# Six buffers of split weights and the two parts of a normed input, placed at other SBUF addresses

## The chip, the cores and the metric

The kernel runs on one core of one Trainium2 chip. The metric is device microseconds (us) of one execution; lower is better. The kernel before takes 1207.95 us, the median of three runs (1205.56 to 1208.57). All data are float32, and the output has to agree with a float32 reference.

## What is computed

One decoder layer on 512 tokens of 1024 features, with a memory of 256 tokens. The reference, cut to its skeleton:

```python
def mixing_sublayer(h, mem_n, ...):
    z = h @ w_in                                  # 1024 -> 9472 columns
    xa, ga, q, k, v, us, xq, gates = jnp.split(z, SPLIT_IDX, axis=-1)
    ya = rg_lru_branch(xa, ga, ...)               # conv, gates, linear scan
    yb = dilated_attention(q, k, v)               # 3 groups of 4 heads
    yc = s5_branch(us, ...)                       # complex diagonal SSM, GLU
    yx = memory_cross_attention(xq, mem_n, mem_wkv)
    g = jax.nn.sigmoid(gates.reshape(B_, L, N_BRANCH, D_MODEL))
    m = (g[:, :, 0] * (ya @ proj_a) + g[:, :, 1] * (yb @ proj_b)
         + g[:, :, 2] * (yc @ proj_c) + g[:, :, 3] * (yx @ proj_x))
    return m @ w_out
def conv_gated_mlp(h, w_up, conv_w, conv_b, w_down):
    up = h @ w_up                                 # 1024 -> 6144
    gate = causal_dwconv(up[..., D_FF:], conv_w, conv_b)
    return (up[..., :D_FF] * jax.nn.gelu(gate)) @ w_down
# reference: x = x + rms_norm(mixing(rms_norm(x))); x = x + rms_norm(mlp(rms_norm(x)))
```

## The kernel before

**Exact products from two parts.** Every large matrix product is made of float32 operands that are split into a high part, rounded to the width of one TensorE pass (type float32r), and a low part, the rest. A product of 128 output features by 512 tokens over a 128-wide slice of the contraction is three matmuls: high weights by low input, high weights by high input, low weights by high input. `mm3` (L82 to L92) writes them in this order for each of 8 slices (6 for a 768-wide contraction), so that a *unit* is 24 (or 18) matmuls of 512 columns into one PSUM bank. In `mm3` the stationary operand, which TensorE loads before a matmul, is a 128x128 slice of the weights, and the moving operand, which it streams, is a 128x512 slice of the input.

**Weights.** `wfetch` (L70) lets SyncE's queue bring 512 KB of weights into a buffer `wraw`. `wload` (L75) makes the two parts: ScalarE copies them to `whi` (L79) and VectorE subtracts (L80) to give `wlo`. Each of the three has three buffers, which rotate, in the pool `wp`; so there are six buffers of split weights, of 128 partitions x 4096 bytes.

**Inputs.** The normed input, turned so that features are on partitions, is `hT`: two tiles `hTh` and `hTl` of 8 x 512 tokens (L178). All 74 units of `w_in` read it as moving operand (names xa, ga, us, xq, q, k, v and gate in the rows). The branches' outputs `ya`, `yx`, `gy`, `yc`, `yb` are pairs of such tiles as well; `merge` (L269) takes them through the projections (prj), each after the unit of its gate: a tile of `merge` is 24 + 18 matmuls (24 + 6 for `yb`). The GLU of the S5 branch reads `gy`. The MLP's first product (`up`, L779) reads `h2h` and `h2l`. Its second (`dn`, L837) turns the roles round: the stationary operand is a slice of `aTh` or `aTl`, and the moving one the split weights; the same holds of `w_out` (`wo`, L699).

**Order.** The program's instructions are written in one order for all engines and each engine runs its own in that order; buffers that come free release the next transfer or copy. Small tiles of 128x512 come from a ring `t2` of six buffers.

**Addresses.** A tile gets its address from its pool when the program is built: pools stand one behind the other in each partition's SBUF, in steps of 32 bytes. The addresses below are read from the built programs, in bytes within a partition, modulo 512. A unit's slices are 512 bytes (weights) and 2048 bytes (input) apart, so a whole tile has one such residue.

Of the kernel before, what the change touches and what calls it, by code (L numbers as in the profile page):

```python
# [12 lines left out]
F32 = mybir.dt.float32  # L13
F32R = mybir.dt.float32r
# [4 lines left out]
PSUM = bass.MemoryType.PSUM  # L19
# [31 lines left out]
def _body(ctx, tc, nc, D):  # L51
    cp = ctx.enter_context(tc.tile_pool(name="cp", bufs=1))
    wp = ctx.enter_context(tc.tile_pool(name="wp", bufs=3))
    ps = ctx.enter_context(tc.tile_pool(name="ps", bufs=4, space=PSUM))
# [19 lines left out]

    def wload(src, n, raw=None):  # L75
        raw = wfetch(src, n) if raw is None else raw
        hi = wp.tile([128, 1024], F32R, tag="whi", name="whi")
        lo = wp.tile([128, 1024], F32R, tag="wlo", name="wlo")
        S.copy(hi[:, :n], raw[:, :n])  # L79
        V.tensor_tensor(out=lo[:, :n], in0=raw[:, :n], in1=f32(hi[:, :n]), op=ALU.subtract)  # L80
        return hi, lo

    def mm3(out, w, x, nk):
        """out[128, N] = sum over nk chunks of w_k^T x_k, operands given as exact hi + lo parts."""
        whi, wlo = w
        n = 0
        for k in range(nk):
            sl = slice(k * 128, (k + 1) * 128)
            for a, b in ((whi, 1), (whi, 0), (wlo, 0)):
                last = PE.matmul(out, a[:, sl], x[b][:, k], start=(n == 0), stop=(n == 3 * nk - 1))  # L90
                n += 1
        return last  # L92

    def split(hi, lo, src, scale=None, eng=V):
        """hi + lo = src (* scale), hi rounded to the width of one pass."""
        if scale is None:
            a = S.copy(hi, src)
            b = eng.tensor_tensor(out=lo, in0=src, in1=f32(hi), op=ALU.subtract)  # L98
        else:
            a = S.activation(hi, src, AF.Identity, scale=scale)  # L100
            b = V.scalar_tensor_tensor(out=lo, in0=src, scalar=scale, in1=f32(hi), op0=ALU.mult, op1=ALU.subtract)
        return a, b
# [11 lines left out]
    def rstd_of(pool, s0, s1, n, tag, bufs=1, between=None, eng=V):  # L114
        """((s0 + s1) / DM + EPS) ** -0.5, with a Newton step after the table's root; between() goes beside the root."""
        t, y, e, r = (pool.tile([128, n], F32, tag=tag + x, name=tag + x, bufs=bufs) for x in "tyer")
        if s1 is None:
            eng.tensor_scalar(out=t, in0=s0, scalar1=EPS * DM, scalar2=None, op0=ALU.add)
        else:
            eng.tensor_scalar(out=t, in0=s0, scalar1=s1, scalar2=EPS * DM, op0=ALU.add, op1=ALU.add)  # L120
        S.activation(y, t, AF.Sqrt, scale=1.0 / DM)
        if between is not None:
            between()
        V.reciprocal(y, y)
        if n == 1:
            eng.tensor_scalar(out=e, in0=y, scalar1=y, scalar2=t, op0=ALU.mult, op1=ALU.mult)
        else:
            eng.tensor_tensor(out=e, in0=y, in1=y, op=ALU.mult)
            eng.tensor_tensor(out=e, in0=e, in1=t, op=ALU.mult)
        eng.tensor_scalar(out=e, in0=e, scalar1=-0.5 / DM, scalar2=1.5, op0=ALU.mult, op1=ALU.add)  # L130
        eng.tensor_tensor(out=r, in0=y, in1=e, op=ALU.mult)
        return r
# [28 lines left out]
    def turned_rows(xs, gain, dst, k0, k1):  # L161
        """dst[k] (hi, lo) <- xs turned to have features on partitions, times gain."""
        for k in range(k0, k1):
            b = axb("nT")
            for t in range(4):
                PE.transpose(b[:, t * 128:(t + 1) * 128], xs[t][:, k * 128:(k + 1) * 128], ident)
            last = split(dst[0][:, k, :], dst[1][:, k, :], b, scale=gain[:, k:k + 1])
        return last

    mp = ctx.enter_context(pool("mp"))  # L170
    # the memory's keys of a head's whole chunks (0 .. 3) and, with the other head's rows at zero, shared ones (4 .. 7)
# [6 lines left out]
    hT = (hp.tile([128, KC, L], F32R, name="hTh"), hp.tile([128, KC, L], F32R, name="hTl"))  # L178
# [16 lines left out]
    with pool("np") as npool:  # L195
# [9 lines left out]
        # the rows' scale comes after the products  # L205
# [14 lines left out]
        ones, dg = npool.tile([128, 128], F32, name="ones"), npool.tile([128, 2, 128], F32, name="dg")  # L220
# [65 lines left out]
    ya = ynew("ya")  # L286
    with pool("lru", bufs=2) as lp, pool("lruc") as lc:
# [5 lines left out]
        with tc.issue_after(normed[0].ins), tc.issue_after(normed[1].ins):  # L293
            for b in (ba, bx):
                V.tensor_scalar(out=b, in0=b, scalar1=0.5, scalar2=None, op0=ALU.mult)
            # softplus(-lam) = max(-lam, 0) + log1p(e), e = exp(-|lam|), by the series of 2 atanh(e / (2 + e))
# [152 lines left out]
    apx = ExitStack()  # L449
    ap = apx.enter_context(pool("at"))  # L450
    sel0 = ap.tile([2, 128], F32, name="selh")
# [4 lines left out]
    # order of the tokens in a group: 4 tiles of 128  # L456
# [12 lines left out]
    class Attention:  # L469
        """Two heads of each group."""  # L470

        def __init__(self, h2):
# [7 lines left out]
            # maxima in columns 0 and 1, sums in 32 and 33  # L480
# [20 lines left out]
        def units_k(self, g):  # L501
            b = unit(U_K + 2 * g + self.h2, "k")
            # each head's keys, the other head's rows at zero
# [63 lines left out]
        def weigh(self):  # L567
            # weights of the groups, per head and token: exp(m_g - M) / sum_g exp(m_g - M) l_g
# [40 lines left out]
        def run(self, fill, before=None):  # L609
            """The group's steps between products that don't wait for them; before() comes with the first."""  # L610
# [69 lines left out]
    with pool("wo") as wo:  # L680
# [93 lines left out]
        # the first products of the MLP in halves of the tokens, the first of which are there sooner  # L774
# [69 lines left out]
    # the last products by tiles of tokens, whose weights stand where h2 did  # L844
# [32 lines left out]
def s5_params(nc, tc, D, keep_pool, pool):  # L877
    V, S = nc.vector, nc.scalar
    r = {}
    with pool("s5t") as tp:  # L880
# [29 lines left out]
        def exp(o, x):  # L910
            """exp(x) = 2^n exp(r): the power of two from the table, rid of its error by its mantissa's bits, times a polynomial."""
# [31 lines left out]
        # z = (A - 1) / lambda  # L943
# [26 lines left out]
        # powers of A  # L970
# [8 lines left out]
        # a chunk's decay, and the powers 0 .. 15 and 0, 16 .. 112 of its rotation  # L979
# [25 lines left out]
class S5:  # L1005
    """S5 in batches of eight groups (four pairs) over 128 chunks of 4 tokens: lanes are (group of the pair, state)."""
# [12 lines left out]
    def tables(self, i):  # L1019
        """The rotations R^c of the chunks, and V_j = A^(3 - j) B."""  # L1020
# [33 lines left out]
    def prepare(self, i):  # L1054
        """The batch's matrices: inputs to chunk sums, states to outputs, inputs to outputs within a chunk."""
# [7 lines left out]
        # inputs: [(j, group of the pair, h), pair, chunk]  # L1063
# [3 lines left out]
        # W_n = C A^n  # L1067
# [14 lines left out]
        # K_tau = Re(C A^tau B), tau = 0 .. 3, with D on its first diagonal  # L1082
# [55 lines left out]
    def states(self, i):  # L1138
        """The batch's states before each chunk."""
# [7 lines left out]
        # sums of a chunk's inputs, turned back by its rotation  # L1147
# [19 lines left out]
        # states before each chunk  # L1167
# [12 lines left out]
    def outputs(self, i):  # L1180
        """GELU of the batch's outputs, chunks on partitions."""
        S, PE, st = self.nc.scalar, self.nc.tensor, self.b[i]
        U, (xr, xi) = st["U"], st["x"]
        # y: [chunk, pair, (group, j, h)]
# [9 lines left out]
    def turned(self, i):  # L1194
        """The same with features on partitions, tokens in (j, c) order, in a bank of PSUM."""
# [70 lines left out]
```

## Time and profile before

| what | before |
|---|---|
| median of three runs | 1207.95 us |
| span of the profiled execution | 1209.4 us |
| PE busy, share of the span | 1181.5 us, 98% |
| DVE, ACT, POOL busy | 685.4, 516.8, 132.4 us |
| granted TensorE clock, mean | 0.995 |
| DMA, mean | 99 GB/s |

The span of the profiled execution lies 1.45 us above the median of the runs. Engines: PE is TensorE (PEld its weight loads), DVE VectorE, ACT ScalarE, POOL GpSimd, SP SyncE. Matmuls overlap, and the end of one is modelled, so its duration (0.39 us here) says little. What it costs is the *gap* from its start to the start of the next one, which this text reads from the start times in the timeline.

### The profile page before, as it was taken

To read this page: it belongs to the slowest core of one execution; us is meant where nothing else is said; L and a number is where in the kernel's file an instruction comes from. 1 tells how busy PE (TensorE), PEld (TensorE's weight loads), DVE (VectorE), ACT (ScalarE), POOL (GpSimd) and SP (SyncE) were. 2 spreads that over 40 slices of the span, in tenths; PEclk is the share of its full clock that TensorE was granted. 3 is DMA by queue.
4 is the path that set the end of the run, shared out by engine and by line. 5 is a ranking of instruction groups with operands and counts; after the bars stand their busy time and mean duration, and the time that the engine had idled before them with its cause. 6 is when DMAs were issued, how large, how long until landed. Compare 5 with 4: busy or idle time off the path is not lost.

```text
span 1209.4 us, 15139 instructions
## 1 busy us (share of the span) xinstructions
PE 1181.5 (98%) x5778; PEld 970.7 (80%) x5778; DVE 685.4 (57%) x1246; ACT 516.8 (43%) x871; POOL 132.4 (11%) x172
## 2 busy tenths in 40 slices
PE   7999999999999999999999999999999999999997
PEld 7877788877787887878888888888888888888886
DVE  5756795688797634485447455475445444432224
ACT  5669833553334235443533233455343443421122
POOL 3200100096561000000000000010000000000000
PEclk9999999999999999999999999999999999999999
DMA  6432252122323322213122324613322223223221
GB/s 244 166 105 70 92 180 76 31 83 78 92 76 100 112 90 66 84 62 122 62 79 75 92 92 134 236 37 105 104 89 91 102 87 103 90 89 102 88 87 69
DMA packets 43720, 119.16 MB, mean 99 GB/s; under 512 B 9566, under 2 KB 13744, under 8 KB 43648
## 3 DMA queue, kind: packets, MB, share of 16 engines
q1 hardware_dynamic: 42000, 114.69, 28.6%
q0 software_dynamic: 1072, 2.46, 0.7%
q8 instruction: 45, 0.74, 0.2%
q10 hardware_dynamic: 576, 1.05, 0.2%
q14 instruction: 27, 0.22, 0.1%
HBM read 114.17 MB, written 4.01 MB: 98 GB/s over the span
## 4 chain that ended last, share of the span: by engine, by line
PE 82%; DVE 9%; ACT 4%; DMA 2%; POOL 1%; issue 1%; SPq 0%; DVEq 0%; ACTq 0%; POOLq 0%
PE up L779 22%; PE gate L90 13%; PE dn L837 11%; PE prj L90 7%; PE v L90 3%; PE k L90 3%; PE q L90 3%; PE us L90 3%; PE xq L90 3%; PE glu L90 2%; PE ga L90 2%; DVE wlo L80 1%; PE kv L90 1%; PE kv L257 1%; PE xs L378 1%
## 5 line engine op out<-in xcount | busy, mean ns | idle before, releaser
L80 DVE TENSOR_TENSOR wlo<-wraw,whi 128x1024 fp32r<-128x1024 f32 (+1 forms) x198 | 230.5, 1166 | 290.4 <-ACT whi L79 282.0
L79 ACT CAST whi<-wraw 128x1024 fp32r<-128x1024 f32 (+1 forms) x198 | 194.3, 984 | 455.3 <-PE up L779 110.7
L779 PE MATMUL up<-h2l,whi 128*128 128x512 f32 (+1 forms) x400 | 152.7, 382 | 1.0 <-DVE h2l L98 1.0
L779 PE MATMUL up<-h2h,whi 128*128 128x512 f32 (+1 forms) x400 | 152.6, 381 | 0.0
L779 PE MATMUL up<-h2h,wlo 128*128 128x512 f32 (+1 forms) x400 | 152.5, 381 | 0.0
L90 PE MATMUL gate<-hTl,whi 128*128 128x512 f32 x256 | 101.2, 395 | 0.0
L90 PE MATMUL gate<-hTh,whi 128*128 128x512 f32 x256 | 100.2, 392 | 0.0
L90 PE MATMUL gate<-hTh,wlo 128*128 128x512 f32 x256 | 100.0, 391 | 0.0
L779 PEld LDWEIGHTS up<-h2l,whi 128*128 128x128 f32 x400 | 75.1, 188 | 17.6 <-DVE h2l L98 1.5
L779 PEld LDWEIGHTS up<-h2h,whi 128*128 128x128 f32 x400 | 75.1, 188 | 16.2
L779 PEld LDWEIGHTS up<-h2h,wlo 128*128 128x128 f32 x400 | 75.1, 188 | 16.0
L837 PE MATMUL dn<-whi,aTh 128*128 128x512 f32 x160 | 63.2, 395 | 0.0
L837 PE MATMUL dn<-whi,aTl 128*128 128x512 f32 x160 | 63.2, 395 | 0.0
L837 PE MATMUL dn<-wlo,aTh 128*128 128x512 f32 x160 | 63.2, 395 | 0.0
L90 PEld LDWEIGHTS gate<-hTl,whi 128*128 128x128 f32 x256 | 48.1, 188 | 10.1 <-issue 0.5
L90 PEld LDWEIGHTS gate<-hTh,wlo 128*128 128x128 f32 x256 | 48.1, 188 | 10.0 <-DVE wlo L80 0.2
L90 PEld LDWEIGHTS gate<-hTh,whi 128*128 128x128 f32 x256 | 48.1, 188 | 9.5
L828 DVE TENSOR_TENSOR fc<-fc,up 128x512 f32<-128x512 f32 x24 | 16.5, 689 | 44.8 <-PE up L779 43.5
L825 DVE SCALAR_TENSOR_TENSOR fc<-gs,fcw,fc 128x512 f32<-128x512 f32 x48 | 36.1, 751 | 0.8
L837 PEld LDWEIGHTS dn<-wlo,aTh 128*128 128x128 f32 x160 | 30.0, 188 | 7.3
L837 PEld LDWEIGHTS dn<-whi,aTh 128*128 128x128 f32 x160 | 30.0, 188 | 7.3
L837 PEld LDWEIGHTS dn<-whi,aTl 128*128 128x128 f32 x160 | 30.0, 188 | 7.3
(520 smaller groups left out, 2566.3 us busy)
## 6 DMA issues: line engine op xcount, KB each, us to landing
wraw<-w_in SPq DMA_DIRECT2D x74, 512.0 KB, 3.5
wraw<-ffn_w_up SPq DMA_DIRECT2D x48, 512.0 KB, 3.5
wraw<-ffn_w_down SPq DMA_DIRECT2D x24, 512.0 KB, 3.4
wraw<-proj SPq DMA_DIRECT2D x24, 384.0 KB, 3.0
wraw<-ssm_glu SPq DMA_DIRECT2D x12, 384.0 KB, 2.9
wraw<-w_out SPq DMA_DIRECT2D x8, 512.0 KB, 4.2
wraw<-mem_wk SPq DMA_DIRECT2D x6, 512.0 KB, 6.5
wraw<-mem_wv SPq DMA_DIRECT2D x6, 512.0 KB, 3.4
```

The lines of the kernel that those rows point to most:

```text
L79: S.copy(hi[:, :n], raw[:, :n])
L80: V.tensor_tensor(out=lo[:, :n], in0=raw[:, :n], in1=f32(hi[:, :n]), op=ALU.subtract)
L90: last = PE.matmul(out, a[:, sl], x[b][:, k], start=(n == 0), stop=(n == 3 * nk - 1))
L257: done = PE.matmul(bv[t][:, :256], mT[a][:, 4 * kh + k, t * 128:(t + 1) * 128], w[:, cs], start=(kh == 0 and k == 0 and o == 0), stop=(kh ...
L378: PE.matmul(b[:, j * 256:(j + 1) * 256], xq[:, x, ch, t * 128:(t + 1) * 128], kx[:, y, i], start=(n == 0 and o == 0), stop=(n == 1 and o = ...
L779: PE.matmul(b[:, cs], a[:, sl], x[:, k, cs], start=(k == 0 and n == 0), stop=(k == KC - 1 and n == 2))
L825: V.scalar_tensor_tensor(out=c, in0=gs[:, j:j + 512], scalar=fcw[:, i, j:j + 1], in1=c, op0=ALU.mult, op1=ALU.add)
L828: V.tensor_tensor(out=c, in0=c, in1=bv, op=ALU.mult)
L837: PE.matmul(acc[t, nh], aT[a][:, k, ts_], b[:, cs], start=(k == 0 and n == 0), stop=(k == 23 and n == 2))
```

## The change

The six buffers leave the rotating pool `wp` for a pool `wq` with a tag of its own for each, 1040 elements wide instead of 1024, so that each begins 4160 bytes after the one before it, 64 bytes further modulo 512. `hTh` and `hTl` get 8 elements more, which moves `hTl` by 32 bytes. Two small tiles move into the ring `t2`: `ones`, and `selh`, which GpSimd's queue loads and ScalarE rounds to `selr`. Everything that is allocated behind these tiles moves with them. Comments are taken out, which shifts line numbers (L90 becomes L94, L779 becomes L783, L837 becomes L841).

```diff
+    wq = ctx.enter_context(tc.tile_pool(name="wq", bufs=1))
...
+    turn = [0]
+
     def wload(src, n, raw=None):
         raw = wfetch(src, n) if raw is None else raw
-        hi = wp.tile([128, 1024], F32R, tag="whi", name="whi")
-        lo = wp.tile([128, 1024], F32R, tag="wlo", name="wlo")
+        i = turn[0] = (turn[0] + 1) % 3
+        hi = wq.tile([128, 1040], F32R, tag="whi%d" % i, name="whi")
+        lo = wq.tile([128, 1040], F32R, tag="wlo%d" % i, name="wlo")
         S.copy(hi[:, :n], raw[:, :n])
         V.tensor_tensor(out=lo[:, :n], in0=raw[:, :n], in1=f32(hi[:, :n]), op=ALU.subtract)
-        return hi, lo
+        return hi[:, :1024], lo[:, :1024]
...
-    hT = (hp.tile([128, KC, L], F32R, name="hTh"), hp.tile([128, KC, L], F32R, name="hTl"))
+    hT = tuple(hp.tile([128, KC * L + 8], F32R, name="hT" + s)[:, :KC * L].rearrange("p (k t) -> p k t", k=KC) for s in "hl")
...
-        ones, dg = npool.tile([128, 128], F32, name="ones"), npool.tile([128, 2, 128], F32, name="dg")
+        ones, dg = t2("ones")[:, :128], npool.tile([128, 2, 128], F32, name="dg")
...
-    sel0 = ap.tile([2, 128], F32, name="selh")
+    sel0 = t2("selh")[0:2, :128]
```

Addresses modulo 512, as built:

| tile | before | after |
|---|---|---|
| `whi`, three buffers | 384, 384, 384 | 384, 0, 128 |
| `wlo`, three buffers | 384, 384, 384 | 448, 64, 192 |
| `hTh`, `hTl` | 384, 384 | 256, 288 |
| `ya`, `yx`, `gy`, `yc` (both parts) | 384 | 256 |
| `yb` | 64 | 0 |
| `h2h`, `h2l` (MLP's input) | 416 | 416 |
| `aTh`, `aTl` (MLP's middle) | 256 | 128 |
| `wlh`, `wll` (weights of the last 96 matmuls of `dn`) | 416 | 416 |
| `weh`, `wel` (one unit's weights) | 480 | 480 |
| `xpTh`, `xpTl`; `vxh`, `vxl` (cross-attention) | 384; 480 | 256; 480 |
| `mm0`, `mm1`; `woh`, `wol` (`w_out`) | 384; 384 | 256; 256 |

While a matmul streams its moving operand, TensorE loads the stationary operand of the next one. The *difference* below is the address of the one minus that of the other, modulo 512:

| matmuls of 512 columns | count | difference before | difference after |
|---|---|---|---|
| units of `w_in` on `hT` | 1776 | 0 | 416, 320, 384; 288, 192, 256; 160, 64, 128 |
| projections of `ya`, `yx`, `yc`; GLU on `gy` | 648 | 0 | 384, 320, 384; 256, 192, 256; 128, 64, 128 |
| `up`, 44 units | 1056 | 32 | 32, 480, 32; 416, 352, 416; 288, 224, 288 |
| `dn` with `wlh`, `wll` | 96 | 160 | 288 |
| `dn` with the six buffers | 480 | 128 | 320, 256, 256; 448, 384, 384; 64, 0, 0 |

Three triples belong to the three rotating pairs of buffers.

On each engine the instructions stand in the same order in both programs, but for `selh` and `selr`. On ScalarE, between the S5 branch and the attention, where `gl` is the S5 output's GeLU and `th` the tanh of a gate, the rounding of `selh` stands in the kernel before like this:

```order
L79 CAST whi<-wraw 128x1024
L1192 ACTIVATE gl<-y_4054 128x512
L454 CAST selr<-selh 2x128
L79 CAST whi<-wraw 128x1024
L273 ACTIVATE th<-gate 128x512
```

In the changed kernel, at the same place on ScalarE:

```order
L1196 ACTIVATE gl<-y_4057 128x512
L83 CAST whi<-wraw 128x1024
L277 ACTIVATE th<-gate 128x512
L458 CAST selr<-selh 2x128
L83 CAST whi<-wraw 128x1024
```

The rounding comes two instructions later. On GpSimd, whose queue loads `selh` and the attention's tables `ab`, and which clears the columns `col`, the load stands before all of them in the kernel before:

```order
L452 DMA selh<-selh 2x128
L477 DMA ab_4147<-ab 128x512
L477 DMA ab_4149<-ab 128x256
L477 DMA ab_4151<-ab 128x256
L482 MEMSET col 128x408
```

In the changed kernel it stands behind the first three of these loads and the clearing:

```order
L481 DMA ab_4154<-ab 128x256
L486 MEMSET col 128x408
L456 DMA selh<-selh 2x128
L481 DMA ab_5078<-ab 128x512
L481 DMA ab_5080<-ab 128x256
```

## Rows read from the trace of the kernel before

**Rows 1.** The page: span, PE's busy time, granted clock in 40 slices, chain by engine.
```profile
span 1209.4 us, 15139 instructions
...
PE 1181.5 (98%) x5778; PEld 970.7 (80%) x5778; DVE 685.4 (57%) x1246; ACT 516.8 (43%) x871; POOL 132.4 (11%) x172
...
PEclk9999999999999999999999999999999999999999
...
PE 82%; DVE 9%; ACT 4%; DMA 2%; POOL 1%; issue 1%; SPq 0%; DVEq 0%; ACTq 0%; POOLq 0%
```

**Rows 2.** Who waited for whom, PE: us in total, times, longest us.
```profile
PE mT L209 <- DMA nkx<-mem: 4.5, 1, 4.5
...
PE prj L90 <- DVE wlo L80: 2.0, 1, 2.0
```

**Rows 3.** The page's DMA issues: out<-in engine op xcount, KB each, us to landing.
```profile
wraw<-w_in SPq DMA_DIRECT2D x74, 512.0 KB, 3.5
...
wraw<-ffn_w_down SPq DMA_DIRECT2D x24, 512.0 KB, 3.4
```

**Rows 4.** Timeline of PE, merge tiles: start us, us, engine line op out<-in.
```profile
643.86 0.47 PE L90 MATMUL gate<-hTl,whi 128*128 128x512 f32 x1
...
691.68 0.50 PE L600 MATMUL bc<-wr,selr 2*128 2x512 f32 x1
```

**Rows 5.** Timeline of PE, up: 24 matmuls apart.
```profile
1010.33 0.40 PE L779 MATMUL up<-h2l,whi 128*128 128x512 f32 x1
...
1015.93 0.39 PE L779 MATMUL up<-h2l,whi 128*128 128x512 f32 x1
```

**Rows 6.** Timeline of PE, dn: 24 matmuls apart.
```profile
1119.99 0.39 PE L837 MATMUL dn<-whi,aTl 128*128 128x512 f32 x1
...
1125.59 0.39 PE L837 MATMUL dn<-whi,aTl 128*128 128x512 f32 x1
```

**Rows 7.** Timeline of PE, the last products of dn, on wl: 24 matmuls apart.
```profile
1179.72 0.40 PE L837 MATMUL dn<-wll,aTh 128*128 128x512 f32 x1
...
1185.35 0.40 PE L837 MATMUL dn<-wll,aTh 128*128 128x512 f32 x1
```

**Rows 8.** Timeline of PE, merge tiles of yb: six of prj, then 24 of gate.
```profile
733.19 0.40 PE L90 MATMUL prj<-ybl,whi 128*128 128x512 f32 x1
...
734.59 0.39 PE L90 MATMUL gate<-hTl,whi 128*128 128x512 f32 x1
...
735.97 0.39 PE L90 MATMUL gate<-hTl,whi 128*128 128x512 f32 x1
...
740.05 0.39 PE L90 MATMUL prj<-ybl,whi 128*128 128x512 f32 x1
```

**Rows 9.** Timeline of PE, cross-attention: six of xo.
```profile
211.15 0.39 PE L405 MATMUL xo<-xpTl,vxh 128*128 128x512 f32 x1
...
212.55 0.28 PE L378 MATMUL xs<-kx,xq 128*128 128x256 f32 x1
```

**Rows 10.** Timeline of PE, matmuls of 256 columns: kv, up with whi, up with weh.
```profile
37.29 0.28 PE L257 MATMUL kv<-wlo,mTh 128*128 128x256 f32 x1
...
37.89 0.28 PE L257 MATMUL kv<-whi,mTl 128*128 128x256 f32 x1
...
815.78 0.28 PE L779 MATMUL up<-h2l,whi 128*128 128x256 f32 x1
...
818.60 0.28 PE L779 MATMUL up<-h2l,weh 128*128 128x256 f32 x1
...
820.99 0.28 PE L779 MATMUL up<-h2l,weh 128*128 128x256 f32 x1
```

**Rows 11.** Timelines of POOL and ACT around selh and selr; [idle before <-releaser].
```profile
395.12 0.46 POOL L482 MEMSET col<- 128x408 f32 x1
...
421.24 0.28 ACT L454 CAST selr<-selh 2x128 fp32r<-2x128 f32 x1
426.01 1.05 ACT L79 CAST whi<-wraw 128x1024 fp32r<-128x1024 f32 x1 [4.49 <-PE gate L90]
```

## The prediction

> **What bounds the kernel now.** I read the page first: PE is busy 98% of the span, the chain that ended last lies on PE for 82% of it, and the granted clock stands in its top tenth in all 40 slices, so TensorE runs at 2.4 GHz [rows 1]. The list of PE's waits says how much a better order could give: the longest, for the first memory tile, is 4.5 us, the longest for split weights is 2.0 us, both once [rows 2]. So the time is the number of matmuls times the gap between their starts. The change touches neither number nor order of matmuls; it can act through that gap alone.
>
> The timeline gives the gap, and the reader should see that it has two levels. From the first gate matmul at 643.86 to the row at 691.68 there are five merge tiles of 24 + 18 = 210 matmuls: 47.82 us / 210 = 227.7 ns [rows 4]. In `up`, 24 matmuls take 1015.93 - 1010.33 = 5.60 us, 233.3 ns each [rows 5]. In `dn`, 24 take 1125.59 - 1119.99 = 5.60 us, 233.3 ns again, and in its last products on `wl` 1185.35 - 1179.72 = 5.63 us, 234.6 ns [rows 6, 7]. Same width, same clock, PE never idle in between.
>
> **What separates the levels.** The table of addresses offers a cause: where the gap is 227 ns, moving operand and next weights differ by 0 modulo 512; in `up` by 32, in `dn` by 128, on `wl` by 160. Those stages differ in much else, so I looked for both levels side by side. In the merge of `yb` the projection differs by 192 and its gate by 0, with the same buffers, the same copies on ScalarE and VectorE and the same queue: six of `prj` take 734.59 - 733.19 = 1.40 us, 233.3 ns each, and the last 18 of the gate that follows take 740.05 - 735.97 = 4.08 us, 226.7 ns each [rows 8]. The cross-attention's `xo`, with weights that no copy writes at the time, differs by 416: six take 1.40 us, 233.3 ns each [rows 9]. So 32, 128, 160, 192 and 416 all sit at 233.3 to 234.6, and 0 at 226.7. One more thing shows in [rows 8]: the first six gate matmuls behind a projection still take (735.97 - 734.59) / 6 = 230 ns each. The fast level needs a run of equal differences to settle.
>
> **The change, part by part.** *The units on `hT` and on the branches' outputs.* These are 74 units of `w_in` [rows 3] by 24 matmuls = 1776, plus 24 tiles of projection by 18 = 432 without the eight of `yb`, plus 12 GLU units by 18 = 216: 2424 matmuls that all have difference 0 now. After the change none has it; their differences are 64, 128, 160, 192, 256, 288, 320, 384 and 416, and they alternate from matmul to matmul, so no run can settle. For 128, 160, 192 and 416 there are rows. For 64, 256, 288, 320 and 384 there is none; the nearest stand on both sides (32 and 128; 192 and 416) and agree, so I take 233.3 for all. Cost: 2424 x (233.3 - 227.7) = 13.6 us; 227.7 is the mean over five whole tiles with their unsettled starts, while the settled 226.7 would make it 16.0 us.
>
> Bounds. Of nine pairs (three weight buffers, three matmuls each) four on `hT` and three on the other inputs have a difference with a row: 1776 x 4/9 + 648 x 3/9 = 1005 matmuls, so 5.6 us of the 13.6 rest on rows. For the rest the rows at half the width give the lower end: `kv` with difference 0 takes 0.60 us / 5 = 120 ns, `up` with 32 (818.60 - 815.78) / 24 = 117.5, and `up` with `weh`, difference 448, (820.99 - 818.60) / 21 = 113.8 [rows 10]. So a difference can be better than 0 by 6.2 ns and better than 32 by 3.7. The upper end is another step of the 6.6 ns between the two levels, up to 240.
>
> *`up`, 1056 matmuls.* Its input stays at 416, one of three weight pairs stays at 32 and 480, the others go to 416, 352 and 288, 224. 233.3 before, 233.3 after for all with a row; nothing is taken. If 480, next to 448, were a step faster it would be a ninth of 1056 x 6.6 ns, 0.8 us. *`dn`, 480 matmuls.* A third of its weight pairs gets 0 for two matmuls of three: 107 x 6.6 = 0.7 us at most, and with the third matmul at 64 in between I count on none of it; nor on the 48 of `yb`, 0.3 us at most. *The memory's keys and values*, 288 matmuls of 256 columns, leave 0, where half width is slowest: 288 x 2.5 ns = 0.7 us to gain at most, much of it in a stretch that waits for data; left out. `w_out` keeps 0.
>
> *`selh` and `selr`.* On GpSimd the load stands behind the clearing of `col`, which ends at 395.6 us; on ScalarE the rounding comes two instructions later than 421.24, behind a copy that starts at 426.01 [rows 11]. That leaves some 30 us for a small load, where the first-listed weight transfers land in 3.5 us [rows 3]. Queued behind it on ScalarE are the copies of weights, which waited 4.49 us for PE there: a rounding of 0.28 us vanishes in that. Without this cover it would cost 0.28 us once. `ones` in the ring changes which buffer is reused, not an instruction. Other engines' work is the same.
>
> *What the slower matmuls hide.* Where PE waits for VectorE, a slower PE waits less. The longest such wait is 2.0 us [rows 2]; I take 1 us off for all of them.
>
> **Sum.** 13.6 - 1.0 = 12.6 us on the profiled 1209.4, which makes a span of 1222.0. The median of the runs lies 1.45 us below the span, so 1207.95 + 12.6 = 1220.5 us, 1.0% slower. With the settled 226.7 and no wait hidden it is 1224; with the small gains of `up`, `dn` and the memory (2.2 us) 1218.
>
> **Rivals.**
>
> *Faster: the differences that have no row are the good ones.* For it speaks 448 at half width, better than 0. Give 64, 256, 288, 320, 384 and, in `up` and `dn`, also 224, 352, 448 and 480 a gap one step under the fast level, 220. Of the 2424, 1005 go up (+5.6 us) and 1419 down by 7.7 ns (-10.9). In `up` four ninths keep rows (32 and 416), so 587 go down by 13.3 ns (-7.8); in `dn` 373 do (-5.0) and 107 go to 226.7 (-0.7). Sum -18.8 us: 1189.2. A gain of 0.3% needs about half of this. Against it: every difference with a row at full width, from 32 round to 416, stands at the slow level.
>
> *No change: the gap doesn't hang on addresses.* The trace shows TensorE's gap change between two neighbouring units [rows 8]; it could be the stage's history that sets the level, with the address a bystander, and then the time stays: 1208. The Trainium skill (SBUF — State Buffer, section Who interferes with whom) is on this side: TensorE has two read ports of its own, one for the moving operand and one for the weights, independent, and never waits for anyone. By that rule no placement matters and the sum is 0. The trace doesn't agree: 233.3 and 226.7 alternate with the difference, tile after tile. Against this rival too: the level returns after each `yb` projection.
>
> *Slower by more: mixed differences cost another step.* If alternating differences put every one of the 2424 at 240 and `up` and `dn` too, it is 2424 x 12.3 + 1536 x 6.7 = 40 us; half of that would be 1228. No row shows a mean gap over 234.6 at this width.
>
> **How the numbers follow.** A measurement of this kernel can tell about 0.3% (3.6 us) from no change. Forecast (1214 to 1226): 0.66. Slower by more: 0.07. Faster rival, whole or in part: 0.14. No change, within 3.6 us, where half-good differences cancel the loss or the address is a bystander: 0.13. So slower 0.73, same 0.13, faster 0.14. The range leaves out the faster half of the first rival and the slower half of the last: 1203 to 1228.
>
> **What would show it.** In the profile after: the gap in merge tiles, five of which took 47.82 us, should make 49.0 us for 210 matmuls, without an idle PE; `up` and `dn` should stay at 233.3 ns. Durations of the copies at L79 and L80 and the list of waits should stay as they are. I am wrong if merge tiles stay at 227.7 ns (then the second rival holds), if some weight buffers give units under 226 ns (the first), or if PE shows a new wait, around 426 us for ScalarE above all, which would mean that the moved load wasn't hidden.

## The result and the profile after

The changed kernel takes 1215.03 us, the median of six runs (1212.17 to 1215.72); beside it on the same chip the kernel before takes 1208.57 us (six runs, 1205.56 to 1211.24). The ratio of the times is 1.0054, with a 95% interval of 1.0034 to 1.0074: slower by 6.5 us, more than the 0.3% that a measurement can tell. In every run on record the device time lies 1.8 us above the span of the same execution. The profiled execution of after is the fastest of its runs, 2.9 us under their median, while that of before, at about 1211.2 us, is 2.7 us over its median. So the spans, 1209.4 and 1210.4 us, understate the difference by some 5.5 us; gaps are read from the two traces, the sum is compared with the medians.

The page of after, answering to [rows 1]: span, busy times, granted clock by slice, chain by engine, and the two copies that fill the weight buffers (busy us, mean ns | idle before).

```profile
span 1210.4 us, 15140 instructions
...
PE 1184.7 (98%) x5778; PEld 967.1 (80%) x5778; DVE 685.4 (57%) x1246; ACT 516.9 (43%) x871; POOL 133.0 (11%) x172
...
PEclk9999999999999999999999999999999999999999
...
PE 83%; DVE 8%; ACT 3%; DMA 2%; POOL 2%; issue 1%; SPq 0%; DVEq 0%; ACTq 0%; POOLq 0%
...
L84 DVE TENSOR_TENSOR wlo<-wraw,whi 128x1024 fp32r<-128x1024 f32 (+1 forms) x198 | 230.2, 1164 | 292.5 <-ACT whi L83 284.0
L83 ACT CAST whi<-wraw 128x1024 fp32r<-128x1024 f32 (+1 forms) x198 | 194.3, 984 | 459.8 <-PE up L783 112.5
```

The same two copies on the page of before, at L80 and L79:

```profile
L80 DVE TENSOR_TENSOR wlo<-wraw,whi 128x1024 fp32r<-128x1024 f32 (+1 forms) x198 | 230.5, 1166 | 290.4 <-ACT whi L79 282.0
L79 ACT CAST whi<-wraw 128x1024 fp32r<-128x1024 f32 (+1 forms) x198 | 194.3, 984 | 455.3 <-PE up L779 110.7
```

Number of matmuls, clock and the other engines' work are as before, and the copies take 984 and 1164 ns where they took 984 and 1166: whoever writes the buffers notices nothing. The list of PE's waits, answering to [rows 2], has the same wait at its head, and the one for split weights is shorter:

```profile
PE mT L213 <- DMA nkx<-mem: 4.4, 1, 4.4
PE yT L1202 <- ACT gl L1196: 3.0, 2, 1.8
...
PE prj L94 <- DVE wlo L84: 1.5, 1, 1.5
```

The second line is longer than in before, where it is 1.5 us. Its two waits are at 287 and 370 us, long before `selr`, and the kernel below without the padding, which takes the time of before, has 3.1 us there; so it isn't what the change costs. What moved is the gap. PE's timeline of after has the five merge tiles of [rows 4], then a matmul of `up` every 24 matmuls, as in [rows 5], and two of `dn` 72 matmuls apart, for [rows 6]:

```profile
646.17 0.48 PE L94 MATMUL gate<-hTl,whi 128*128 128x512 f32 x1
...
695.15 0.50 PE L604 MATMUL bc<-wr,selr 2*128 2x512 f32 x1
```
```profile
999.80 0.39 PE L783 MATMUL up<-h2h,whi 128*128 128x512 f32 x1
...
1005.36 0.40 PE L783 MATMUL up<-h2h,whi 128*128 128x512 f32 x1
...
1010.92 0.39 PE L783 MATMUL up<-h2h,whi 128*128 128x512 f32 x1
...
1016.46 0.39 PE L783 MATMUL up<-h2h,whi 128*128 128x512 f32 x1
```
```profile
1109.74 0.40 PE L841 MATMUL dn<-whi,aTl 128*128 128x512 f32 x1
...
1126.42 0.40 PE L841 MATMUL dn<-whi,aTl 128*128 128x512 f32 x1
```

The five tiles take 48.98 us in place of 47.82, 233.2 ns a matmul. The three units of `up` take 5.56, 5.56 and 5.54 us, 231.4 ns in the mean, and the 72 matmuls of `dn` 16.68 us, 231.7 ns: both a little *faster* than the 233.3 of before.

Over the whole trace, every gap between consecutive starts goes to its group; gaps of more than 262 ns (150 at 256 columns) are waits and are set apart. Mean gaps in ns:

| group | matmuls | before | after | gaps, us |
|---|---|---|---|---|
| units of `w_in` | 1776 | 227.6 | 232.7 | +9.1 |
| projections (without `yb`) and GLU | 648 | 227.4 | 232.0 | +3.0 |
| `up`, 512 columns | 1056 | 233.3 | 231.4 | -2.0 |
| `dn` (without `wl`) | 480 | 233.3 | 231.7 | -0.8 |
| memory's keys and values, 256 columns | 288 | 119.9 | 118.0 | -0.5 |
| sum | | | | +8.8 |

The medians differ by 6.5 us, 2.3 less than the gaps. The interval of the ratio puts it at 4.1 to 8.9 us, so the 2.3 alone would prove little. The waits bear them out: over all of PE's matmuls, what the gaps set apart have over their group's mean comes to 40 to 43 us in the traces of the five kernels whose `w_in` gap is 227.5 to 227.6 ns, and to 36 to 38 us in the four with 231.8 to 232.7 ns that keep all products and their order. A slower PE waits less.

### The profile page after: what moved, and what is told of

Its sections match the earlier page's. It is cut to its first block, busy times and chain, and to the rows that moved or that the text cites. A ratio compares the mean times of both kernels' runs of the same rounds, so it can differ in the third digit from the quotient of the medians.

```text
span 1210.4 us, 15140 instructions
## 1 busy us (share of the span) xinstructions
PE 1184.7 (98%) x5778; PEld 967.1 (80%) x5778; DVE 685.4 (57%) x1246; ACT 516.9 (43%) x871; POOL 133.0 (11%) x172
## 4 chain that ended last, share of the span: by engine, by line
PE 83%; DVE 8%; ACT 3%; DMA 2%; POOL 2%; issue 1%; SPq 0%; DVEq 0%; ACTq 0%; POOLq 0%
PE up L783 22%; PE gate L94 12%; PE dn L841 11%; PE prj L94 7%; PE v L94 3%; PE k L94 3%; PE us L94 3%; PE xq L94 3%; PE q L94 3%; PE glu L94 2%; PE ga L94 2%; PE xa L94 2%; PE kv L94 1%; DVE wlo L84 1%; PE kv L261 1%
## 5 line engine op out<-in xcount | busy, mean ns | idle before, releaser
L84 DVE TENSOR_TENSOR wlo<-wraw,whi 128x1024 fp32r<-128x1024 f32 (+1 forms) x198 | 230.2, 1164 | 292.5 <-ACT whi L83 284.0
L783 PE MATMUL up<-h2l,whi 128*128 128x512 f32 (+1 forms) x400 | 152.6, 382 | 1.3 <-DVE h2l L102 1.3
L783 PE MATMUL up<-h2h,wlo 128*128 128x512 f32 (+1 forms) x400 | 151.6, 379 | 0.0
L783 PE MATMUL up<-h2h,whi 128*128 128x512 f32 (+1 forms) x400 | 151.6, 379 | 0.0
L94 PE MATMUL gate<-hTl,whi 128*128 128x512 f32 x256 | 102.3, 400 | 0.0
L94 PE MATMUL gate<-hTh,wlo 128*128 128x512 f32 x256 | 101.3, 396 | 0.0
L94 PE MATMUL gate<-hTh,whi 128*128 128x512 f32 x256 | 101.2, 395 | 0.0
L783 PEld LDWEIGHTS up<-h2l,whi 128*128 128x128 f32 x400 | 75.1, 188 | 16.9 <-DVE h2l L102 1.7
L783 PEld LDWEIGHTS up<-h2h,wlo 128*128 128x128 f32 x400 | 75.1, 188 | 15.8
L783 PEld LDWEIGHTS up<-h2h,whi 128*128 128x128 f32 x400 | 75.1, 188 | 15.2
L841 PE MATMUL dn<-whi,aTh 128*128 128x512 f32 x160 | 63.0, 394 | 0.0
L841 PE MATMUL dn<-wlo,aTh 128*128 128x512 f32 x160 | 63.0, 394 | 0.0
L841 PE MATMUL dn<-whi,aTl 128*128 128x512 f32 x160 | 62.8, 393 | 0.0
L94 PEld LDWEIGHTS gate<-hTh,wlo 128*128 128x128 f32 x256 | 48.2, 188 | 11.1 <-DVE wlo L84 0.2
L94 PEld LDWEIGHTS gate<-hTl,whi 128*128 128x128 f32 x256 | 48.1, 188 | 11.0 <-issue 0.5
L94 PEld LDWEIGHTS gate<-hTh,whi 128*128 128x128 f32 x256 | 48.2, 188 | 10.7
L841 PEld LDWEIGHTS dn<-whi,aTl 128*128 128x128 f32 x160 | 30.0, 188 | 7.1
L841 PEld LDWEIGHTS dn<-wlo,aTh 128*128 128x128 f32 x160 | 30.0, 188 | 7.1
L841 PEld LDWEIGHTS dn<-whi,aTh 128*128 128x128 f32 x160 | 30.0, 188 | 6.9
```

Of the source, the lines that this page charges most:

```text
L783: PE.matmul(b[:, cs], a[:, sl], x[:, k, cs], start=(k == 0 and n == 0), stop=(k == KC - 1 and n == 2))
L841: PE.matmul(acc[t, nh], aT[a][:, k, ts_], b[:, cs], start=(k == 0 and n == 0), stop=(k == 23 and n == 2))
```

## The experiments

All edits are to the changed kernel unless said otherwise. Each run's kernel before was measured beside it: 1208.1 to 1208.7 us in every group of runs. Gaps are the means of the table's kind.

### The padding alone taken back

```diff
-        hi = wq.tile([128, 1040], F32R, tag="whi%d" % i, name="whi")
-        lo = wq.tile([128, 1040], F32R, tag="wlo%d" % i, name="wlo")
+        hi = wq.tile([128, 1024], F32R, tag="whi%d" % i, name="whi")
+        lo = wq.tile([128, 1024], F32R, tag="wlo%d" % i, name="wlo")
...
-    hT = tuple(hp.tile([128, KC * L + 8], F32R, name="hT" + s)[:, :KC * L].rearrange("p (k t) -> p k t", k=KC) for s in "hl")
+    hT = (hp.tile([128, KC, L], F32R, name="hTh"), hp.tile([128, KC, L], F32R, name="hTl"))
```

> The changed kernel with its padding alone taken back: the six weight buffers are 1024 columns wide again and the two parts of the normed input stand side by side, while the buffers still rotate by hand in a pool of their own and the two small tiles keep their new places. Theory A (the gap between matmul starts is set by the difference of addresses modulo 512 between a matmul's moving operand and the next one's stationary operand, 226.7 ns at a steady 0): all 2424 differences are 0 again, the w_in units go back from 232.7 to 227.6 ns and the projections and GLU from 232.0 to 227.4 ns, and the kernel to 1208.5 us, ratio 0.999 to 1.001. Rival B (the pool of the buffers or the two moved tiles cost the time): the gaps stay at 232 to 233 ns and the time at 1215 us, ratio 1.004 to 1.006.

Measured: 1207.55 us, ratio 0.9994 (0.9986 to 1.0003); `w_in` 227.6 ns, projections and GLU 227.3. The five merge tiles:

```profile
639.59 0.47 PE L94 MATMUL gate<-hTl,whi 128*128 128x512 f32 x1
...
687.41 0.50 PE L604 MATMUL bc<-wr,selr 2*128 2x512 f32 x1
```

47.82 us, to the hundredth that of before. The new pool, the rotation by hand and the two moved tiles cost nothing that these runs can tell; the addresses are the whole cost. Rival B falls.

### The six buffers alone, the low input alone

Of the diff above, the first of these kernels takes back only the second part (the input), the other only the first part (the buffers).

> The changed kernel with the two parts of the normed input side by side again: only the six weight buffers are staggered. Theory A: the w_in, projection and GLU matmuls alternate between two nonzero differences (384 and 320, 256 and 192, 128 and 64), so the w_in units stay at 232 to 233 ns and the projections at 232 ns, and the time at 1215 us, ratio 1.004 to 1.007. Rival C (it is the 32 bytes between the two parts of the input that cost, since they alternate from matmul to matmul): the w_in units fall back to 227.6 ns, 1776 x 5.1 ns = 9 us less than in the changed kernel, and the time to 1206 to 1210 us.

> The changed kernel with six buffers at one residue again: only the low part of the normed input is moved by 32 bytes. In a w_in unit the differences are then 32, 0, 0 in turn, in the projections and GLU 0 throughout. Theory A1 (each matmul's gap goes by its own difference): a third of the w_in matmuls rise to about 233 ns, mean 229.5 ns, 592 x 5.6 ns = +3.3 us, time 1210 to 1212 us. Theory A2 (226.7 ns needs an unbroken run of zero differences): all 1776 rise to about 231 to 233 ns, +6 to +10 us of gaps, time 1212 to 1217 us. Both: projections and GLU at 227.4 ns. Rival C (as above, the 32 bytes between the parts are the whole cost): as A2, and more than the staggered buffers alone.

Measured: with the buffers alone 1213.64 us, 1.0044 (1.0032 to 1.0056), `w_in` 232.3 ns, projections and GLU 232.3. With the low input alone 1213.78 us, 1.0045 (1.0032 to 1.0058), `w_in` 231.8 ns, projections and GLU 227.6. So the buffers alone give most of the cost (5.0 of 6.5 us), and rival C falls. The low input alone gives as much (5.1 us): the two don't add up.

The other kernel is the sharper one. In its units the differences are 32, 0, 0 in turn. If each matmul paid for itself the mean would be 229.5 ns; it is 231.8, and even the matmuls at 0 take 229.3 and 231.7 ns. A nonzero difference spoils its neighbours too (theory A2).

It also showed something I had not asked for. The projections of `yb` stand there at a constant difference of 256, and take 227.5 ns where 192 took 233.4 before: 256 seems as good as 0.

### All differences made zero

The kernel before, with two pads:

```diff
+    cp.tile([128, 8], F32, name="pad")
     half = cp.tile([128, 2], F32, name="half")
...
+    fp.tile([128, 32], F32, name="pad2")
     aT = tuple(fp.tile([128, 24, L], F32R, name="aT" + s) for s in "hl")
```

> The kernel before with two pads: one of 32 bytes ahead of everything on the left of the memory, which moves the weights from 384 to 416 modulo 512, where the moving operand of the up products stands, and one of 128 bytes ahead of the gated activations, which brings them to 416 too. The w_in, projection and GLU products keep their difference of 0. Theory A: the up products (1056 matmuls) and the down products (480 and 96) go from 233.3 ns to 226.7 to 227.6 ns: 1632 x 6 ns = -9.8 us, less about 0.5 us for the 192 products of 256 columns, which go from 117.5 to 120 ns; time 1199 us, between 1198 and 1203 us if waits take some of it, ratio 0.991 to 0.996. Rival D (the address is a bystander, the stage or its operands set the gap): up and down stay at 233 ns and the time at 1208.5 us.

Measured: 1198.47 us (1197.21 to 1200.6), ratio 0.9921 (0.9909 to 0.9933). `up` and `dn` in its timeline, each pair of rows 120 matmuls apart:

```profile
999.79 0.39 PE L780 MATMUL up<-h2l,whi 128*128 128x512 f32 x1
...
1026.99 0.39 PE L780 MATMUL up<-h2l,whi 128*128 128x512 f32 x1
```
```profile
1109.73 0.39 PE L839 MATMUL dn<-whi,aTl 128*128 128x512 f32 x1
...
1136.93 0.39 PE L839 MATMUL dn<-whi,aTl 128*128 128x512 f32 x1
```

27.20 us for 120 matmuls, 226.7 ns in both, where both took 233.3. 160 bytes of padding make the kernel before 10.2 us faster. The gap is set by placement, not by the stage or its operands: rival D falls, and with it the prediction's rival that the address is a bystander. The sum of gaps is -10.5 us here (7.0 in `up`, 3.2 in `dn`, 0.7 on `wl`, +0.4 at 256 columns), and almost all of it is time, since these stages have no waits that would give it back.

### The gap at every difference

The two parts of the input unpadded, two buffers for the raw weights in place of three, and an offset for each weight tile. The kernel's own time, 1221.22 us in its one run, isn't compared; its gaps are.

```diff
+OFF = [8 * i for i in range(16)] + [1, 2, 4, 127]
...
-        i = turn[0] = (turn[0] + 1) % 3
-        hi = wq.tile([128, 1040], F32R, tag="whi%d" % i, name="whi")
-        lo = wq.tile([128, 1040], F32R, tag="wlo%d" % i, name="wlo")
+        turn[0] += 1
+        i, o = turn[0] % 3, OFF[turn[0] % len(OFF)]
+        hi = wq.tile([128, 1152], F32R, tag="whi%d" % i, name="whi")
+        lo = wq.tile([128, 1152], F32R, tag="wlo%d" % i, name="wlo")
+        hi, lo = hi[:, o:o + 1024], lo[:, o:o + 1024]
```

> One look at the gap by difference. Both split buffers of a weight tile are read from the same offset, which stays for the whole unit and is another for each unit in turn: 0 to 480 bytes in steps of 32, then 4, 8, 16 and 508 bytes (buffers 1152 columns wide; two buffers for the raw weights in place of three, so the time of the kernel itself is not to be compared). Within a unit the difference is then one constant. Theory A (226.7 ns at a steady 0 alone): one group of units at 226.7 ns, those at offset 0, and all others at 231 to 234 ns, the differences of 4 to 16 bytes among them. Theory A256 (what counts is the difference modulo 256, as the projections of the branch with a difference of 256 at 227.5 ns in the run with the low input alone moved suggest): the units at offsets 0 and 256 at 226.7 ns, the rest at 231 to 234 ns. Theory A64 (a small distance inside one 64-byte piece is still a hit): the units at 4 to 16 bytes at 226.7 ns too. Rival D (the address is a bystander): all offsets at one gap, 227 ns in the w_in units.

Ten `w_in` units in a row, PE never waiting; each row is the first matmul of a unit, so the next row less this one is 24 gaps. Their constant differences are 320, 288, 256, 224, 192, 160, 128, 96, 64 and 32.

```profile
145.71 0.40 PE L98 MATMUL us<-hTl,whi 128*128 128x512 f32 x1
...
151.21 0.40 PE L98 MATMUL us<-hTl,whi 128*128 128x512 f32 x1
...
156.81 0.39 PE L98 MATMUL us<-hTl,whi 128*128 128x512 f32 x1
...
162.26 0.39 PE L98 MATMUL us<-hTl,whi 128*128 128x512 f32 x1
...
167.85 0.40 PE L98 MATMUL us<-hTl,whi 128*128 128x512 f32 x1
...
173.45 0.39 PE L98 MATMUL xq<-hTl,whi 128*128 128x512 f32 x1
...
179.06 0.40 PE L98 MATMUL xq<-hTl,whi 128*128 128x512 f32 x1
...
184.66 0.39 PE L98 MATMUL xq<-hTl,whi 128*128 128x512 f32 x1
...
190.26 0.40 PE L98 MATMUL xq<-hTl,whi 128*128 128x512 f32 x1
...
195.77 0.40 PE L98 MATMUL xq<-hTl,whi 128*128 128x512 f32 x1
...
201.37 0.39 PE L98 MATMUL xq<-hTl,whi 128*128 128x512 f32 x1
```

Units of 5.60 us (233.3 ns) are the rule; three stand out, 5.45 us at 256 and 5.50 and 5.51 at 320 and 64. The means inside the units of `up`, some 46 gaps or more for each, say the same with no start in them:

| difference modulo 256 | 0 | 32 | 64 | 96 | 128 | 160 | 192 | 224 |
|---|---|---|---|---|---|---|---|---|
| `up`, below 256 | 226.7 | 233.4 | 229.4 | 233.4 | 233.5 | 233.9 | 233.4 | 233.1 |
| `up`, from 256 | 226.7 | 233.3 | 229.3 | 233.5 | 233.5 | 233.9 | 233.4 | 233.1 |

`w_in`, projections and `dn` give the same curve within 1.3 ns, except for `w_in` at 0, 228.8. Its period is 256 bytes, not 512, and it has a second, shallower dip at 64. Theory A256 holds but for this dip. Small distances lie in between (16 bytes: 228.3 ns in `up`), so A64 doesn't hold as put; rival D falls again.

### The same stagger in steps of 256 bytes

To make room, a small tile of the memory's norms (`dg`) moves into the ring `t2`, here and in the four kernels after this one.

```diff
-        hi = wq.tile([128, 1040], F32R, tag="whi%d" % i, name="whi")
-        lo = wq.tile([128, 1040], F32R, tag="wlo%d" % i, name="wlo")
+        hi = wq.tile([128, 1024 + 64 * (i < 2)], F32R, tag="whi%d" % i, name="whi")
+        lo = wq.tile([128, 1024], F32R, tag="wlo%d" % i, name="wlo")
...
-    hT = tuple(hp.tile([128, KC * L + 8], F32R, name="hT" + s)[:, :KC * L].rearrange("p (k t) -> p k t", k=KC) for s in "hl")
+    hT = tuple(hp.tile([128, KC * L + 64 * (s == "h")], F32R, name="hT" + s)[:, :KC * L].rearrange("p (k t) -> p k t", k=KC) for s in "hl")
```

> The changed kernel with its stagger made in steps of 256 bytes in place of 64 and 32: two of the high weight buffers and the high part of the normed input are 64 columns wider, the other parts unpadded, so that weights and input stand at 384 or 128 modulo 512, and the differences in w_in units and projections are a mix of 0 and 256 (a small diagonal tile is moved to the pool of the transposed tiles to make room). Theory A256 (the gap goes by the difference modulo 256, period 256 in the sweep): w_in units 227.6 ns and projections and GLU 227.4 ns, time 1208.5 us, ratio 0.999 to 1.001. Theory A (modulo 512, as in the prediction): a mix of zero and nonzero differences, about 232 ns, time 1213 to 1216 us.

Measured: 1208.34 us, ratio 0.9998 (0.9988 to 1.0008); `w_in` 227.6 ns, projections and GLU 227.2. The five merge tiles:

```profile
642.98 0.47 PE L94 MATMUL gate<-hTl,whi 128*128 128x512 f32 x1
...
690.80 0.50 PE L604 MATMUL bc<-wr,selr 2*128 2x512 f32 x1
```

47.82 us once more, with differences that alternate between 0 and 256. Mixing is harmless where all of them are 0 modulo 256.

### Which stationary operand counts

The next four ask whether the moving operand must agree with its own weights or with those loaded for the next matmul. In all four, high and low parts stand 128 bytes apart modulo 256. This is the edit of the first three; the last one pads the high input in place of the low one, with the high part first:

```diff
-        hi = wq.tile([128, 1040], F32R, tag="whi%d" % i, name="whi")
-        lo = wq.tile([128, 1040], F32R, tag="wlo%d" % i, name="wlo")
+        hi = wq.tile([128, 1056], F32R, tag="whi%d" % i, name="whi")
+        lo = wq.tile([128, 1024 + 32 * (i > 0)], F32R, tag="wlo%d" % i, name="wlo")
...
-    hT = tuple(hp.tile([128, KC * L + 8], F32R, name="hT" + s)[:, :KC * L].rearrange("p (k t) -> p k t", k=KC) for s in "hl")
+    hT = tuple(hp.tile([128, KC * L + 32 * (s == "l")], F32R, name="hT" + s)[:, :KC * L].rearrange("p (k t) -> p k t", k=KC) for s in "lh")[::-1]
```

The first two differ in the order of the three products alone; this is the second's:

```diff
-            for a, b in ((whi, 1), (whi, 0), (wlo, 0)):
+            for a, b in ((wlo, 0), (whi, 0), (whi, 1)):
```

> All high parts (weights and normed input) at one residue modulo 256 and all low parts 128 bytes from it, the three products of a chunk in the order of the changed kernel: high weights with low input, high with high, low with high. Next-stationary reading (what counts is a matmul's moving operand against the stationary operand of the matmul after it, loaded beside it): differences 128, 128, 0 in turn in the w_in units, mean 231 to 233 ns. Own-stationary reading (the moving operand against the weights that it meets): differences 128, 0, 128, also 231 to 233 ns. Both: w_in + projections about +9 and +3 us of gaps, time 1212 to 1217 us. This one is the other half of the next.

> The same addresses as the run before it, with the three products of a chunk in another order: low weights with high input, high with high, high weights with low input. Next-stationary reading: the moving operand and the stationary operand of the matmul behind it now always stand at the same residue, the differences are 0, 0, 0, so the w_in units fall to 227 to 228 ns, 1776 x 4 to 5 ns = 7 to 9 us less than in the run before it. Own-stationary reading: 128, 0, 128 in turn, the w_in units stay at 231 to 233 ns and the time as in the run before it, 1212 to 1217 us.

Measured: 1215.57 us (1.0065, 1.005 to 1.0081) and 1220.86 us (1.0105, 1.009 to 1.012); `w_in` 232.1 and 231.2 ns. The second has every moving operand at the residue of the next weights, and isn't fast: the next-stationary reading, which is the prediction's, falls in this form. Its 5.3 us more come from its order, not from its gaps: it asks first for the low weights, which VectorE makes from the high ones. In its list of waits:

```profile
PE kv L94 <- DVE wlo L84: 4.7, 3, 3.1
...
PE gate L94 <- DVE wlo L84: 2.2, 2, 2.0
```

The own-stationary reading would explain both. The last two put it to the test with two products in strict turn in the `w_in` units, which leaves out the product of the high parts there. They differ in the place of the low and the high input alone:

```diff
-                for a, b in ((whi, 1), (whi, 0), (wlo, 0)):
+                for a, b in ([((whi, 1), (wlo, 0))[(3 * k + j) % 2] for j in range(3)] if x is hT else
+                             ((whi, 1), (whi, 0), (wlo, 0))):
```

> Only the gap of the w_in units is asked for: their 24 matmuls are made two products in strict turn, high weights with low input and low weights with high input, so that the product of the high parts is left out there and the output is not the reference's. High weights and high input stand at one residue modulo 256, low weights and low input 128 bytes from it: each moving operand is at the residue of the stationary operand of the next matmul, and 128 bytes from its own. Next-stationary reading: 226.7 to 227.6 ns. Own-stationary reading: 231 to 234 ns. All-alike reading (226.7 ns needs every stationary and moving operand of the stretch at one residue): 231 to 234 ns.

> The same two products in turn (the product of the high parts of the w_in units left out again), with the residues of the low and the high input exchanged: each moving operand is at the residue of its own stationary operand, and 128 bytes from the next one's. Next-stationary reading: 231 to 234 ns. Own-stationary reading: 226.7 to 227.6 ns. All-alike reading: 231 to 234 ns, as in the run before it.

With agreement with the next weights, six units take 33.12 us, 230.0 ns:

```profile
139.81 0.39 PE L95 MATMUL us<-hTl,whi 128*128 128x512 f32 x1
...
172.93 0.39 PE L95 MATMUL xq<-hTl,whi 128*128 128x512 f32 x1
```

With agreement with their own weights, three units in one place take 16.44 us, 228.3 ns, and four in another 22.72 us, 236.7 ns:

```profile
55.17 0.39 PE L95 MATMUL xa<-hTl,whi 128*128 128x512 f32 x1
...
71.61 0.39 PE L95 MATMUL ga<-hTl,whi 128*128 128x512 f32 x1
```
```profile
149.89 0.40 PE L95 MATMUL us<-hTl,whi 128*128 128x512 f32 x1
...
172.61 0.40 PE L95 MATMUL xq<-hTl,whi 128*128 128x512 f32 x1
```

Means over all units: 230.0 and 230.7 ns. Neither agreement alone gives 226.7, so both single readings fall. Of the three the all-alike reading is left, that all operands of the stretch must share a residue; its 231 to 234 ns were a little too high for the first kernel, and the two levels of the second fit none of the three. By which of its reads TensorE meets which other stays open.

### A version with more pads

To the kernel with both pads come three more (64 bytes behind `vx`, 448 ahead of `mT`, 64 in the attention's pool), and `ones` moves into the ring `t2`:

```diff
+    kvp.tile([128, 16], F32, name="pad4")
...
+        npool.tile([128, 112], F32, name="pad3")
...
+    ap.tile([128, 16], F32, name="pad5")
```

> The kernel with up and down products at difference 0, and three pads more: 64 bytes behind the memory's values (their products, 48 matmuls, from 192 to 0 modulo 256), 64 bytes in the attention's pool (the last branch's projections, 48 matmuls, to 0 modulo 256), 448 bytes ahead of the memory's transposed rows (the 288 products of 256 columns from 0 to 448, where the sweep has 114.4 ns against 118 to 120 ns); the tile of ones moves to the pool of the transposed tiles to make room. Expected: 96 x 6.6 ns = -0.6 us, and 288 x 0 to 5 ns = -0 to -1.4 us: 1196.5 to 1198.5 us, ratio to the kernel before 0.990 to 0.992. If placement outside the counted groups mattered, it would lie outside these bounds.

Measured: 1196.34 us (1196.02 to 1196.59), ratio 0.9906 (0.9889 to 0.9922); the ratio lies inside the bounds, the time 0.2 us under them. The projections of `yb` fall from 233.3 to 226.8 ns, `xo` from 232.7 to 230.5 (6.6 ns were expected, and why its six matmuls in a row don't reach 226.7 wasn't tried), the memory's 256-column products from 119.9 to 115.9. It is the fastest kernel here, 11.8 us under the one before, though its gain over two pads (1198.47) isn't more than these runs can tell.

## Why the prediction came out as it did

It forecast 1220.5 us, slower, with 0.73; measured are 1215.0, slower, inside 1203 to 1228. The path was right: the addresses change the gap, and the gap the time. Of the 12.6 us forecast only 6.5 came, about half, because each size was off to the same side.

- **What bounds the kernel: right.** Number, order and clock of the matmuls stayed, and the gap carried the change. The five merge tiles, forecast at 49.0 us, took 48.98.
- **Term 1, 2424 x 5.6 ns = 13.6 us: too large by 1.5.** It is 1776 x 5.1 + 648 x 4.6 = 12.1 us. "I take 233.3 for all" is the step: alternating differences sit at 232.0 to 232.7, not at the level of a constant one. That the five merge tiles agreed to 0.02 us is luck: they lie at 233.2, above the mean of their own groups.
- **The differences without a row: three of five were wrong.** Where they are constant, 64 and 320 are at 229.4 and 229.3 ns and 256 is at 226.7, so the neighbours on both sides, which agreed, were no bound: 32, 128, 192 and 416 are all slow and enclose the three. It did little harm only because the change mixes them: in after, matmuls at 256 take 232.7 ns.
- **Term 2, `up` and `dn` at nothing: off by 2.8 us.** I left out "small gains" of 0.8 and 0.7 us; they are 2.0 and 0.8. In `up` mixes such as 32 and 480 are faster (231.4 over all units) than 32 throughout, which no row of before could show; why they are stays open. The memory's products gained 0.5 of the 0.7 left out. "`w_out` keeps 0" misses 24 of its 192 matmuls, which use the six buffers and go to 384 and 448; that is 0.1 us.
- **Hidden waits, 1 us: too small.** It is 2.3 by the medians. I took the longest wait for VectorE as the measure (the list also has 2.1 us for ScalarE's `whi`), but each stage with waits absorbs. Three more kernels agree: where the gaps of `w_in` grow, 8.2, 6.7 and 10.1 us of gaps (buffers alone, low input alone, low parts shifted) become 5.0, 5.1 and 7.4 us of time, each give or take 1.4 to 1.9; where `up` and `dn` shrink, 10.5 become 10.2.
- **From span to time, 1.45 us: a wrong reading that cancels.** The sum set the span of one execution against the time of others. The forecast is the median of before plus 12.6 all the same.
- **The moved loads: nothing, as forecast.** The rounding of `selr` stands two instructions later on ScalarE and hides; PE has no wait of 0.7 us or more between 372 and 543 us:

```profile
425.52 1.05 ACT L83 CAST whi<-wraw 128x1024 fp32r<-128x1024 f32 x1 [4.75 <-PE gate L94]
426.47 0.59 ACT L277 ACTIVATE th<-gate 128x512 f32<-128x512 f32 x1
426.96 0.28 ACT L458 CAST selr<-selh 2x128 fp32r<-2x128 f32 x1
```

- **The cause: right as a placement, wrong in its form.** That moving operand and next weights differ by 0 modulo 512 has two faults: the period is 256, and agreement with the next weights alone isn't enough. In before, all operands of the fast units stood at one residue, so no row could separate the readings.

Of the rivals, "the gap doesn't hang on addresses" is refuted by the kernel with two pads and by the sweep. The Trainium skill (SBUF — State Buffer, section Who interferes with whom) has the two read ports of TensorE independent; by that rule no pad would matter. The runs don't agree: 160 bytes of padding are worth 10.2 us. The faster rival, that differences without a row are the good ones, had 64, 256 and 320 on its side, but none is better than 0, and mixed, in `w_in` and the projections, they are slower too. "Slower by more" holds for no group of the changed kernel, whose highest mean is 233.3. Gaps above that do occur elsewhere: 236.7 ns in part of one mix, and 239.6 in one `dn` unit of the sweep, at a difference of 132.

## What to carry to other kernels

Where TensorE streams matmuls without a pause, read the gap between starts by stage and set it against the addresses of both operands modulo 256: here, with float32r operands, 512 columns and new weights for each matmul, operands at one residue ran at 226.7 to 229 ns, others at 228 to 240, most at 231 to 234, and a pad of some bytes ahead of a tile moves a whole stage from one to the other. A stagger that is meant to keep buffers apart should go in steps of 256 bytes, which cost nothing here, or it takes a good placement apart. Count such a gain or loss in full only in stages without waits; in stages with waits, a quarter to two fifths of it went into them, as far as medians with intervals of some 2 us either way can tell.

## What the runs showed that I had not expected

- **The curve over the difference.** 226.7 ns at 0 modulo 256, 229.3 at 64, 233.1 to 234 at the other multiples of 32. At 256 columns the best is elsewhere: 115.9 ns with memory and weights 64 bytes apart (differences 448 and 64) against 119.9 at 0. The difference alone doesn't set this gap: 448 gives 113.6 ns in that kernel, where the weights are the stationary operand, and 117.8 in the kernel with the low input alone, where they are the moving one.
- **Two levels at the same addresses.** In the kernel that agrees with its own weights, 53 of the 74 `w_in` units run at about 228 ns and 21 at about 236, with the same residues modulo 256 and the same instructions. Mostly a stretch of units keeps its level (228.3 from 55.17 us on, 236.7 from 149.89 on), but one changes between two units that follow without a pause: 236.7 from 117.76 on, 228.3 from 123.44 on. What sets the level stays open; the unsettled starts of [rows 8] may be the same, which wasn't tried.
- **No placement reached the gaps that the Trainium skill gives.** The Trainium skill (TensorE: Matmul & The Clock Gate, section Back-to-back issue gap) gives, for 512 columns at 2.4 GHz, 512/2.4 + 2.5, some 216 ns, as the gap of an isolated matmul, and some 131 ns for a stream. The runs don't agree: the lowest settled level in any stream here is 226.7.
